# A hybrid encoder layer on one core: the order of all instructions moved from a hand-written interleaving to a list scheduler inside the kernel

## The chip, the cores and the metric

One NeuronCore of a Trainium2 chip runs the whole layer in one launch. The metric is the device time in microseconds (us). The engines are PE (TensorE, matrix products), DVE (VectorE), ACT (ScalarE), POOL (GpSimd) and SP (SyncE, which here only issues DMA transfers). Each engine runs its own instructions in the order in which they stand in the program and waits on semaphores for the others, so an instruction that waits holds up everything that stands behind it on its engine.

## The reference

A residual stream `x` of 256 rows by 4096 goes through one wide projection (16,592 columns). Its columns feed sixteen heads of an attention with a forget gate ("fox"), thirty-two heads of a recurrence ("rwkv"), and a gate; both head groups are gated, joined, projected again, added to the stream and normalised:

```
proj = einsum('bsd,dc->bsc', x, w_in)            # 4096 x 16592 weights
fox_out = softmax attention with summed log-forget gates        # 16 heads of 128
rw = rw + (rw_prev - rw) * mu_shift                              # one step of token shift
S_t = S_{t-1} diag(w_t) + (S_{t-1} a_t) b_t^T + v_t k_t^T ;  y_t = S_t r_t   # 32 heads of 64
h = concat([fox_out, rwkv_out]) * silu(z)
out = einsum('bsc,cd->bsd', h, w_out)            # 4096 x 4096 weights
x = layernorm(ALPHA * x + out, ln_gain, ln_bias)
```

All of it is float32, and the two large weight matrices alone are 339 MB that must come from memory once.

## The kernel before

**The big products.** A float32 product is made of three fast ones. `split` (L137 to L142) writes a weight tile of 128 x 1024 as a rounded high part on ACT (L140, `w...h`) and a remainder on DVE (L141, `w...l`). `mm` (L144 to L148) then multiplies high by high, low by high and high by low: three matmuls of 128x512 for each of two halves of the rows and for each 512 columns of the tile, so twelve matmuls for one weight tile. The high parts have four buffers, the remainders three, the raw tiles four. So the split of tile k+3 cannot write its remainder before PE has finished tile k, and must have written it before PE reaches tile k+3.

**The loops.** A pass n (eight of them) handles two fox heads and four rwkv heads in four blocks b of sixteen weight tiles (`block`, L245). The first block, n=0 and b=0, runs apart at the start with its own loads, together with the small `accl` products. Then comes the output projection, eight blocks b of sixteen tiles (L839 to L853, `oacc`, weight tiles `wo`).

**The small work.** Everything else (token shift, norms, softmax, and for each n the recurrence by chunks) runs as Python generators in the list `sides`. `slot()` moves each of them one step. `block` calls it after every six big matmuls (L254), and `yield` in a generator means "let one slot pass", so the interleaving is written by hand as numbers of slots (`W`, L43). In two other loops slots are taken with no big matmuls between them: while a block is being unloaded (L882), and while a head is not finished (L900). What is issued in such a loop stands in one run in each engine's program.

**The recurrence for one n** (`rwkv`, L505). `gp` (products over 64 rows, on half the array) is masked into `gb`; `gb` goes through memory (`nd`) and comes back as `Nb`; 31 rounds of `prod` (L578, a product) and `xc` (L581, a sum) solve a small triangular system on DVE; `xc` goes through memory (`td`) and comes back as `T`, which four DVE transposes put into `X`. Then for each of four chunks: `rh` on PE, `R` on DVE, `up` on PE (L652), `UV` on ACT, `sp` and `yp` on PE. The products `sp`, `yp`, `rh`, `gp`, `qt` and `xp` use a part of the array as a tile of its own; `up`, `fpt`, `fsp`, `fop`, `lp`, `np`, `vs` and `bkt` use the whole array.

**The order.** The tile framework holds program order where `keep_in_program_order` says so and may move the rest. The splits stand where `weights` (L238) calls `fetch`: at the start of each tile's matmuls it fills up to three tiles ahead.

**The end.** After the last block, `moments(m)` (L960) turns the row statistics into factors: BN_AGGR (L970), a square root on ACT (L972), then on DVE a reciprocal (L973) and four tiny operations up to `zd` (L977), a transpose on PE (`zp`), a copy on ACT, and the last products `wp` (L1001). `gain` (L867) multiplies the last 512 columns; it is issued after `zd` by `tc.issue_after(last)`.

## Time and profile before

| what | value |
|---|---|
| time, median of 3 runs | 1956.07 us (1955.14 to 1956.11) |
| the profiled execution's own time | 1955.92 us |
| its span, first to last instruction | 1954.0 us |
| PE busy | 1935.8 us, 99% |
| PE weight loads | 1585.4 us, 81% |
| DVE, ACT, POOL busy | 1366.9, 978.4, 79.9 us |
| moved by DMA | 420 MB, mean 215 GB/s |
| granted clock of PE, mean | 0.997 |

A row of a time line gives the start, the duration, engine, source line, operation, the tile written and the tiles read, and in brackets how long the engine was idle before it and who ended that. Durations of matmuls overlap, since they are pipelined: what a matmul costs is the distance from its start to the start of the next. `L146` is line 146 of the kernel before. A float32 product on the small side shows as two matmuls in the trace for one in the program.

### The profile page before, as it was taken

To read this page: it belongs to the slowest core of one execution; us is meant where nothing else is said; L and a number is where in the kernel's file an instruction comes from. 1 tells how busy PE (TensorE), PEld (TensorE's weight loads), DVE (VectorE), ACT (ScalarE), POOL (GpSimd) and SP (SyncE) were. 2 spreads that over 40 slices of the span, in tenths; PEclk is the share of its full clock that TensorE was granted. 3 is DMA by queue.
4 is the path that set the end of the run, shared out by engine and by line. 5 is a ranking of instruction groups with operands and counts; after the bars stand their busy time and mean duration, and the time that the engine had idled before them with its cause. 6 is when DMAs were issued, how large, how long until landed. Compare 5 with 4: busy or idle time off the path is not lost.

```text
span 1954.0 us, 28165 instructions
## 1 busy us (share of the span) xinstructions
PE 1935.8 (99%) x10153; PEld 1585.4 (81%) x10153; DVE 1366.9 (70%) x2212; ACT 978.4 (50%) x1485; POOL 79.9 (4%) x111
## 2 busy tenths in 40 slices
PE   9998999999999999999999999999999999999998
PEld 7887888878887888788878887888788878888886
DVE  6588667866886687667857785778577856755555
ACT  6453455455545554565456545644564454433332
POOL 0010001000100010001000100010001000000000
PEclk9999999999999999999999999999999999999999
DMA  9577767867785778677867786777677877866664
GB/s 337 146 235 198 208 167 241 225 194 199 226 234 184 215 213 233 193 219 208 225 195 219 212 226 194 227 211 219 193 228 203 269 259 241 251 199 200 189 198 168
DMA packets 269392, 420.13 MB, mean 215 GB/s; under 512 B 142338, under 2 KB 171028, under 8 KB 269252
## 3 DMA queue, kind: packets, MB, share of 16 engines
q1 hardware_dynamic: 268820, 417.91, 72.8%
q8 instruction: 80, 1.31, 0.3%
q14 instruction: 60, 0.49, 0.1%
q10 hardware_dynamic: 432, 0.43, 0.1%
HBM read 388.61 MB, written 29.64 MB: 214 GB/s over the span
## 4 chain that ended last, share of the span: by engine, by line
PE 95%; DVE 3%; DMA 1%; ACT 0%; issue 0%; DVEq 0%; SPq 0%; ACTq 0%
PE acc L146 24%; PE acc L148 23%; PE acc L147 23%; PE oacc L851 6%; PE oacc L853 6%; PE oacc L852 6%; PE yp L677 1%; PE gp L517 1%; PE up L652 1%; PE rh L625 1%; PE sp L661 0%; DVE xc L581 0%; DVE prod L578 0%; PE fsp L716 0%; PE fop L735 0%
## 5 line engine op out<-in xcount | busy, mean ns | idle before, releaser
L581 DVE TENSOR_REDUCE xc<-prod 128x8 f32<-128x16 f32 (+30 forms) x248 | 73.1, 295 | 7.1
L578 DVE TENSOR_TENSOR prod<-Nb,xc 128x8 f32<-128x8 f32 (+30 forms) x248 | 71.7, 289 | 6.4
L141 DVE TENSOR_TENSOR w_0l<-w,w_0h 128x1024 fp32r<-128x1024 f32 x31 | 38.2, 1232 | 37.7 <-ACT w_0h L140 27.4
L141 DVE TENSOR_TENSOR w_6l<-w,w_6h 128x1024 fp32r<-128x1024 f32 x31 | 39.0, 1258 | 34.8 <-ACT w_6h L140 18.7
L141 DVE TENSOR_TENSOR w_10l<-w,w_10h 128x1024 fp32r<-128x1024 f32 x31 | 37.9, 1224 | 36.1 <-PE acc L148 20.1
L141 DVE TENSOR_TENSOR w_8l<-w,w_8h 128x1024 fp32r<-128x1024 f32 x31 | 37.8, 1219 | 33.7 <-ACT w_8h L140 14.0
L140 ACT CAST w_0h<-w 128x1024 fp32r<-128x1024 f32 x31 | 32.7, 1054 | 55.0 <-DMA w<-in_w_main_dram 35.0
L141 DVE TENSOR_TENSOR w_5l<-w,w_5h 128x1024 fp32r<-128x1024 f32 x31 | 38.4, 1240 | 28.4 <-PE acc L148 17.3
L140 ACT CAST w_7h<-w 128x1024 fp32r<-128x1024 f32 x31 | 32.6, 1052 | 48.3 <-PE acc L147 28.8
L148 PE MATMUL acc<-w_7l,x 128*128 128x512 f32 x124 | 48.6, 400 | 5.8 <-DVE w_7l L141 5.8
L141 DVE TENSOR_TENSOR w_7l<-w,w_7h 128x1024 fp32r<-128x1024 f32 x31 | 37.9, 1222 | 21.9 <-PE acc L148 12.8
L141 DVE TENSOR_TENSOR w_11l<-w,w_11h 128x1024 fp32r<-128x1024 f32 x31 | 37.9, 1223 | 20.5 <-PE acc L148 14.9
L141 DVE TENSOR_TENSOR w_12l<-w,w_12h 128x1024 fp32r<-128x1024 f32 x31 | 37.5, 1211 | 19.5 <-PE acc L148 16.0
L140 ACT CAST w_13h<-w 128x1024 fp32r<-128x1024 f32 x31 | 32.6, 1052 | 37.1 <-DMA w<-in_w_main_dram 17.9
L146 PE MATMUL acc<-w_8h,x 128*128 128x512 f32 x124 | 50.5, 407 | 0.6 <-ACT w_8h L140 0.6
L146 PE MATMUL acc<-w_7h,x 128*128 128x512 f32 x124 | 51.0, 411 | 0.0
L146 PE MATMUL acc<-w_5h,x 128*128 128x512 f32 x124 | 50.5, 408 | 0.0
L141 DVE TENSOR_TENSOR w_14l<-w,w_14h 128x1024 fp32r<-128x1024 f32 x31 | 38.2, 1231 | 17.3 <-issue 10.9
L146 PE MATMUL acc<-w_3h,x 128*128 128x512 f32 x124 | 50.3, 405 | 0.0
L140 ACT CAST w_8h<-w 128x1024 fp32r<-128x1024 f32 x31 | 32.5, 1050 | 34.8 <-DMA w<-in_w_main_dram 24.5
L140 ACT CAST w_10h<-w 128x1024 fp32r<-128x1024 f32 x31 | 32.5, 1047 | 34.8 <-PE acc L147 32.6
L146 PE MATMUL acc<-w_6h,x 128*128 128x512 f32 x124 | 49.9, 402 | 0.0
(813 smaller groups left out, 6527.6 us busy)
## 6 DMA issues: line engine op xcount, KB each, us to landing
w<-in_w_main_dram SPq DMA_DIRECT2D x496, 512.0 KB, 3.9
wo<-in_w_o_dram SPq DMA_DIRECT2D x128, 512.0 KB, 3.8
bt<-bk SPq DMA_DIRECT2D x88, 128.0 KB, 4.2
Nb<-nd SPq DMA_DIRECT2D x16, 512.0 KB, 4.6
wr<-in_w_main_dram SPq DMA_DIRECT2D x15, 512.0 KB, 6.2
hd<-hl SPq DMA_DIRECT2D x29, 256.0 KB, 4.5
h<-hd SPq DMA_DIRECT2D x29, 256.0 KB, 5.6
raw<-bt SPq DMA_DIRECT2D x16, 256.0 KB
```

What stands on the lines that cost most here:

```text
L140: nc.scalar.copy(hi[:, :n], src[:, :n])
L141: nc.vector.tensor_tensor(lo[:, :n], src[:, :n], hi[:, :n].bitcast(F32), ALU.subtract)
L146: nc.tensor.matmul(acc[:, :n], xs[k][:, 0, tt], hi[:, o : o + n], start=(k == 0), stop=False)
L147: nc.tensor.matmul(acc[:, :n], xs[k][:, 1, tt], hi[:, o : o + n], start=False, stop=False)
L148: nc.tensor.matmul(acc[:, :n], xs[k][:, 0, tt], lo[:, o : o + n], start=False, stop=(k == KT - 1))
L517: nc.tensor.matmul(gp[u][j][:, c * P : (c + 1) * P], BK[h, u, c, :], lt[j][h, u, c, :], start=True, stop=True)
L578: first = nc.vector.tensor_tensor(prod[:, :, :, s + 1 :], nb[:, :, s : s + 1, s + 1 :].to_broadcast([P, 2, NJ, w]), xc[:, :, :, s + 1 :], ...
L581: nc.vector.tensor_reduce(xc[:, :, :, s : s + 1], prod[:, :, :, s:], AX.X, ALU.add)
L625: nc.tensor.matmul(rh[HALF[j], u * C : (u + 1) * C], lt[j][:, u, c, 0:C], SV[j][:, u, c, :], start=True, stop=True)
L851: nc.tensor.matmul(acc, ht[k][:, 0, tt], hi, start=(k == 0), stop=False)
L852: nc.tensor.matmul(acc, ht[k][:, 1, tt], hi, start=False, stop=False)
L853: nc.tensor.matmul(acc, ht[k][:, 0, tt], lo, start=False, stop=(k == KT - 1))
```

## The change

Every operation is now noted instead of issued. `nc` becomes an object `Later` whose engines record each call with its operands. `flush` then gives an order: it starts with estimated durations (`span_of`), goes forward in its own estimated time, and lets each engine take, among the operations that are ready and for which a buffer is free, the one with the lowest key. The key is the place in the program; for what `weights` notes (loads and splits of weights) it is lower by 100,000, so that these go first. Small matmuls become ready only 1000 ns after their inputs in the second of three flushes, which holds nearly all of the work. Matmuls that follow each other in the same partial-array tiling are kept together (`batches`). The instructions are then issued in that order, and `keep_in_program_order` holds each of them in it. The operations themselves, their operands, buffers and numbers are the same.

```diff
+SWITCH = 190
+MARGIN = 1000
...
+    def take(self, engine, call, name, args, kwargs):
...
+        op.hold, op.lag = span_of(engine, name, kwargs, outs[0], ins)
...
+        op.key = self.count - self.sooner
...
+        if engine == "tensor":
+            bank = outs[0].tensor.name
+            if bank in self.banks:
+                op.after.add(self.banks[bank])
+            self.banks[bank] = op
...
+    def flush(self, stay=(), closing=None, margin=0):
+        made = [o for o in self.ops]
+        ops, self.ops = self.batches(), []
...
+        def admit(op):
+            op.ready = max([0.0] + [self.seen(o, op) for o in op.after])
+            if op.engine == "tensor" and not op.main:
+                op.ready += margin
+            heapq.heappush(soon[op.engine], (op.ready, op.key, id(op), op))
...
+            _, _, op = heapq.heappop(ready[e])
+            if e == "tensor" and self.mode and op.mode != self.mode:
+                same = [x for x in ready[e] if x[2].mode == self.mode]
+                if same:
...
+            wait = self.places(op)
+            if wait is None:
+                held.append(op)
+                continue
...
+        made.sort(key=lambda o: o.start)
...
+        for op in made:
+            ins = op.call(*op.args, **op.kwargs)
+            self.tc.keep_in_program_order(ins)
...
+    def batches(self):
...
+                if op.mode and last and last.mode == op.mode:
+                    own = {id(o) for o in last.parts}
+                    if not any(any(id(b) in own for b in o.after) for o in op.after if o.engine != "tensor"):
+                        last.parts.append(op)
+                        continue
...
+    def places(self, op):
+        at = 0.0
+        for where in op.touches:
+            if self.left[where][3]:
+                continue
+            free, queue = self.slots[self.left[where][0]]
+            if not free or (len(free) < 5 and queue[0] != where and not self.left[where][0].startswith("ps")):
+                return None
+            at = max(at, free[0])
+        return at
...
-    nc = tc.nc
+    nc = Later(tc)
...
+    nc.flush(closing="_spool")
...
+        nc.sooner = AHEAD
         while len(ready) < 3 and (stream or raws):
             fetch()
+        nc.sooner = 0
...
+            nc.flush([t for _, *hl in ready for t in hl] + [raw for _, raw in raws], "_rp", MARGIN)
...
-    with tc.issue_after(last):
-        gain(0, NB - 1)
+    z0, _ = moments(0)
+    gain(0, NB - 1)
...
+    nc.flush()
```

`span_of` gives each operation an estimated time on its engine and a delay until its result can be used, from its engine, its shape and, for a transfer, its size and the size of its pieces. `admit` adds the margin to every small matmul, also to one whose only predecessor is the matmul before it in the same PSUM bank (`self.banks`).

## The prediction

> **What bounds the kernel now.** The page first: PE is busy nearly all of the span, and the chain that ended last runs along PE.

> ```profile
> span 1954.0 us, 28165 instructions
> ...
> PE 1935.8 (99%) x10153; PEld 1585.4 (81%) x10153; DVE 1366.9 (70%) x2212; ACT 978.4 (50%) x1485; POOL 79.9 (4%) x111
> ...
> PE 95%; DVE 3%; DMA 1%; ACT 0%; issue 0%; DVEq 0%; SPq 0%; ACTq 0%
> ```

> DVE at 70% and ACT at 50% are no bound on the average. So an order can win only what PE spends waiting, what it loses by how small matmuls lie between big ones, and the ends. The waits of PE by releaser say what waiting there is:

> ```profile
> PE acc L148 <- DVE w_7l L141: 5.8, 1, 5.8
> PE zp L989 <- DVE zd L977: 1.4, 1, 1.4
> PE warmup L108 <- POOL idle L105: 1.3, 1, 1.3
> PE acc L146 <- ACT w_8h L140: 0.6, 1, 0.6
> PE acc L148 <- DVE wr2l L141: 0.5, 1, 0.5
> PE oacc L853 <- DVE wo_3l L141: 0.5, 1, 0.5
> ```

> One wait is worth speaking of. PE's time line around it:

> ```profile
> 186.56 0.39 PE L146 MATMUL acc<-w_7h,x 128*128 128x512 f32 x1
> 192.71 0.80 PE L148 MATMUL acc<-w_7l,x 128*128 128x512 f32 x1 [5.75 <-DVE w_7l L141]
> 193.30 0.63 PE L147 MATMUL acc<-w_7h,x 128*128 128x512 f32 x1
> 193.72 0.63 PE L148 MATMUL acc<-w_7l,x 128*128 128x512 f32 x1
> ...
> 198.42 0.56 PE L147 MATMUL acc<-w_8h,x 128*128 128x512 f32 x1
> 198.81 0.40 PE L148 MATMUL acc<-w_8l,x 128*128 128x512 f32 x1
> ```

> After the wait the matmuls start 0.42 us apart. The windows view has the reason: the granted clock.

> ```profile
> 186.00:192.00 6.00, 0.95 (x5) 0.45 (x3) 5.62 (x14) 0.45 (x2) 0.00 (x0) 0.99 0.02 8
> 192.00:199.00 7.00, 6.29 (x15) 5.03 (x16) 3.68 (x5) 5.05 (x8) 0.00 (x0) 0.52 0.65 186
> ```

> The third number from the end of a row is the clock: 0.52 in the seven microseconds after the wait. DVE, which PE waited for, was busy 5.62 of the 6 us, with this between two splits:

> ```profile
> 178.98 1.22 DVE L141 TENSOR_TENSOR w_6l<-w,w_6h 128x1024 fp32r<-128x1024 f32 x1
> ...
> 190.50 0.42 DVE L581 TENSOR_REDUCE xc<-prod 128x8 f32<-128x256 f32 x1
> 190.84 0.68 DVE L564 TENSOR_TENSOR bon<-bon,vv 128x512 f32<-128x512 f32 x1
> 191.43 1.22 DVE L141 TENSOR_TENSOR w_7l<-w,w_7h 128x1024 fp32r<-128x1024 f32 x1
> ```

> For 12 us DVE worked off a run of `prod` and `xc` rounds, because the loop at L882 had issued them without big matmuls and so without splits between.

> **The change part by part.**

> *The splits (first key).* Before, at the end of this run of DVE in pass n=0, block 3 (`w_3_7l` is the remainder of its tile 7):

> ```order
> L578 TENSOR_TENSOR prod_1689<-Nb_1547,xc_1690 128x8x30
> L581 TENSOR_REDUCE xc_1690<-prod_1689 128x8
> L578 TENSOR_TENSOR prod_1689<-Nb_1547,xc_1690 128x8x31
> L581 TENSOR_REDUCE xc_1690<-prod_1689 128x8
> L564 TENSOR_TENSOR bon_1085<-bon_1085,vv_1818 128x512
> L141 TENSOR_TENSOR w_3_7l<-w_3_7_1804,w_3_7h 128x1024
> L141 TENSOR_TENSOR w_3_8l<-w_3_8_1834,w_3_8h 128x1024
> ```

> and now on DVE, the same place:

> ```order
> L358 TENSOR_TENSOR w_3_5l<-w_3_5_1031,w_3_5h 128x1024
> L358 TENSOR_TENSOR prod_1019<-Nb_993,xc_1020 128x8x19
> L358 TENSOR_REDUCE xc_1020<-prod_1019 128x8
> L358 TENSOR_TENSOR prod_1019<-Nb_993,xc_1020 128x8x20
> L358 TENSOR_REDUCE xc_1020<-prod_1019 128x8
> L358 TENSOR_TENSOR prod_1019<-Nb_993,xc_1020 128x8x21
> L358 TENSOR_TENSOR w_3_6l<-w_3_6_1034,w_3_6h 128x1024
> L358 TENSOR_REDUCE xc_1020<-prod_1019 128x8
> L358 TENSOR_TENSOR prod_1019<-Nb_993,xc_1020 128x8x22
> L358 TENSOR_REDUCE xc_1020<-prod_1019 128x8
> L358 TENSOR_TENSOR prod_1019<-Nb_993,xc_1020 128x8x23
> L358 TENSOR_TENSOR w_3_7l<-w_3_7_1038,w_3_7h 128x1024
> ```

> The rounds are spread among the splits. Over the whole program the longest run of other DVE operations between two splits falls from 28 to 11, and the 11 stand once, in the first blocks; elsewhere it is 8. So this wait goes. Its worth: from 186.56 to 192.71 is 6.15 us instead of one interval of 0.227 (rows below), so 5.92; from 192.71 to 198.81 there are fourteen intervals in 6.10 instead of 3.18 us, so 2.92. Together **-8.84 us**. I see nothing late next at this place: `w_3_6l` and `w_3_8l` are no further apart than elsewhere.

> [...]

> *The other small waits.* In the output projection the remainder came late by

> ```profile
> 1685.28 0.39 PE L852 MATMUL oacc<-wo_3h,h 128*128 128x512 f32 x1
> 1686.19 0.50 PE L853 MATMUL oacc<-wo_3l,h 128*128 128x512 f32 x1 [0.53 <-DVE wo_3l L141]
> ```

> 0.91 - 0.23 = 0.68 us, after the row statistics and `gain` of two blocks had been issued in a row; now splits stand between these. **-0.68**. The wait for `w_8h` (0.6) and the one for `wr2l` (0.5) lie in the first 100 us, where the first small chain and the first loads are; the new order has its run of 11 operations there, so I keep them: 0, at best -1.1.

> *The margin, and small matmuls one by one.* The margin also parts matmuls that only share a bank. On PE in pass 2, before, `up` (products of the recurrence) and the big `acc` products:

> ```order
> L148 MATMUL acc_0_1_5751<-w_0_2l,x_285 128x512
> L652 MATMUL up_0_5851<-R_0_5836,X 128x64 x2
> L146 MATMUL acc_0_0_5750<-w_0_2h,x_288 128x512
> L147 MATMUL acc_0_0_5750<-w_0_2h,x_288 128x512
> L148 MATMUL acc_0_0_5750<-w_0_2l,x_288 128x512
> ```

> and now:

> ```order
> L358 MATMUL up_0_1781<-R_0_1776,X 128x64
> L358 MATMUL acc_0_0_1764<-w_0_2l,x_154 128x512
> L358 MATMUL acc_0_1_1765<-w_0_2h,x_154 128x512 x2
> L358 MATMUL acc_0_1_1765<-w_0_2l,x_154 128x512
> L358 MATMUL acc_0_0_1764<-w_0_3h,x_159 128x512
> L358 MATMUL up_0_1781<-R_0_1776,X 128x64
> ```

> The pair has become two, five big matmuls apart. The same happens to `lp`, `np`, `vs`, `fsp`, `fpt`, `fop`, `tr` and, in twos, `bkt`: small matmuls stand in 467 places between big ones, 245 before. The partial-array groups (`gp`, `qt`, `xp`, `rh`, `sp`, `yp`) are whole in both. What a lone one costs against a group, PE's time line shows, since before has a few of both:

> ```profile
> 206.31 0.39 PE L148 MATMUL acc<-w_10l,x 128*128 128x512 f32 x1
> 206.54 0.49 PE L730 MATMUL fpt<-cs,lg 128*128 128x128 f32 x3
> 206.79 0.48 PE L146 MATMUL acc<-w_11h,x 128*128 128x512 f32 x1
> 207.10 0.39 PE L147 MATMUL acc<-w_11h,x 128*128 128x512 f32 x1
> 207.33 0.39 PE L148 MATMUL acc<-w_11l,x 128*128 128x512 f32 x1
> ```

> ```profile
> 399.11 0.39 PE L148 MATMUL acc<-w_10l,x 128*128 128x512 f32 x1
> ...
> 399.79 0.39 PE L148 MATMUL acc<-w_10l,x 128*128 128x512 f32 x1
> 400.02 0.27 PE L730 MATMUL fpt<-cs,lg 128*128 128x128 f32 x1
> 400.05 0.48 PE L146 MATMUL acc<-w_11h,x 128*128 128x512 f32 x1
> 400.37 0.39 PE L147 MATMUL acc<-w_11h,x 128*128 128x512 f32 x1
> ```

> 399.11 to 399.79 are three intervals, so 0.227 each. The three cost 207.33 - 206.31 - 3 x 0.227 = 0.34, that is 0.113 each; the lone one 400.37 - 399.79 - 2 x 0.227 = 0.126. So a place more costs about 0.013 us. With 222 places more: 2.9 us if all cost so; nothing, or 1 us less than nothing, if the 256 and 512 wide ones (`lp`, `np`, `vs`, most of the extra places) lose nothing by standing alone, which no row here settles. I take the middle, **+1.5**, from -1 to +2.9.

> As for the margin itself: `up` stood 6 big matmuls behind `rh` and now stands 8 behind, and the chunks of the recurrence lie further apart. That chain is not on the path, and each pass has room for it: X is made long before `qt` needs it.

> *The end.* `issue_after` is gone. On DVE, before:

> ```order
> L970 BN_AGGR mv_17445<-lst_855 128x2
> L973 RECIPROCAL rs_17447<-sd_17446 128x1
> L974 TENSOR_TENSOR s_17448<-mv_17445,rs_17447 128x1
> L975 CAST zh_17449<-s_17448 128x1
> L976 COPY zd_17450<-zh_17449 128x2
> L977 TENSOR_TENSOR zd_17450<-s_17448,zh_17449 128x1
> L867 TENSOR_TENSOR res_15549<-res_15549,lg_17231 128x512
> ```

> now:

> ```order
> L358 BN_AGGR mv_15900<-lst_839 128x2
> L358 TENSOR_TENSOR res_15549<-res_15549,lg_15857 128x512
> L358 RECIPROCAL rs_15902<-sd_15901 128x1
> L358 TENSOR_TENSOR s_15903<-mv_15900,rs_15902 128x1
> L358 CAST zh_15904<-s_15903 128x1
> ```

> `gain` now fills the gap in which DVE waited for ACT's square root, and is longer than it:

> ```profile
> 1942.59 0.37 DVE L970 BATCH_NORM_AGGREGATE mv<-lst 128x2 f32<-128x48 f32 x1
> 1943.32 0.16 DVE L973 RECIPROCAL rs<-sd 128x1 f32<-128x1 f32 x1 [0.36 <-ACT sd L972]
> ...
> 1944.12 0.68 DVE L867 TENSOR_TENSOR res<-res,lg 128x512 f32<-128x512 f32 x1
> ```

> 0.68 - 0.36 = 0.32 later for the reciprocal and all behind it: `zd`, PE's `zp`, ACT's copy, `wp`. For the second half of the rows that chain is the end of the kernel; for the first half PE reaches its `zp` with nothing to spare, and waits. Nothing needs `gain` earlier. Twice 0.32: **+0.6**; at least one of the two, at most both.

> *Noting, keys and program order* add no instruction: each engine has the same operations. Loads keep their depth of four raw tiles.

> The sum on the profiled execution's own 1955.92 us (span 1954.0 and 1.9 around it, 0.15 under the median): 1955.92 - 8.84 - 0.68 + 1.5 + 0.6 = **1948.5 us**. Its own range: 1955.92 - 8.84 - 0.68 - 1.1 - 1 + 0.3 = 1944.6 below, 1955.92 - 8.84 + 2.9 + 0.6 + 1.5 for small new waits = 1952.1 above.

> **The rivals.** *A wait takes the place of the old one.* In the first block DVE's run of 11 operations waits in turn for PE's first transposes, for ACT's copies and for a table load, and the split of tile 3 of block 1 stands behind it, with PE behind that. If PE idles there for 4 us and the half clock follows for 6.1 us (2.9 lost), 6.9 of the 9.5 us are given back: 1955.4 us. For it: the two waits that are there today. Against it stands the slack of the stretch now:

> ```profile
> 80.00:100.00 20.00, 19.07 (x82) 14.89 (x83) 13.68 (x22) 10.78 (x17) 0.00 (x0) 1.00 0.63 179
> ```

> DVE (the third of the five busy times) is free for 6.3 of the 20 us and ACT, the fourth, for 9.2, so they catch up. 0.13.

> *Slower: `X` waits for `T`.* After the last `xc` of a pass only three splits now stand before the transposes into `X`, where 11 to 16 stood: 3 x 12 x 0.227 = 8.2 us. The trip through memory took

> ```profile
> 396.53 0.90 SPq L588 DMA_DIRECT2D td<-xc  x2
> ...
> 400.93 3.65 SPq L590 DMA_DIRECT2D T<-td  x8
> ```

> ```profile
> T<-td SPq DMA_DIRECT2D x64, 16.0 KB, 1.7
> ```

> 400.93 + 3.65 + 1.7 - 396.53 = 9.75 us, so DVE may stand 1.5 us, and behind it the next split, for which PE waits. That split has two tiles of room, 5.4 us, less its own 1.2: PE waits when the trip passes some 12.4 us. SP is a queue too; the eight `T` loads may stand behind weight loads that wait for buffers. At 16 us PE would lose 3.6 us in each of eight passes, 28.8 us, and the clock with it: 1977 us or more. For it: the order. Against: 9.75. 0.10.

> *A lone small matmul is nearly free.* Its weights load while the big one before it runs. The row at 400.02 shows 0.03 us to the next start. If 0.03 were all, 222 places times 0.08 would give 18 us: 1929 us. The next row speaks against it: the big matmul behind starts 0.32 later instead of 0.227. [...] 0.04.

> That the order stays as it was is excluded: the rows above are the built programs.

> **How the numbers follow.** A measurement of this kernel tells about 0.2% from no change, 3.9 us: faster is under 1952.2, slower over 1960.0. The forecast has 0.73 and lies in faster with the last rival (0.04): 0.77. The moved wait is 0.13 in the middle, the slower rival 0.10. The range leaves out the last two rivals, 0.14: from 1944 to 1958, the upper end for a moved wait a little larger than priced. The forecast's own is 1944.6 to 1952.1.

> **What would show it.** Right: no PE wait over 1 us between 60 and 1900 us, the clock at 1.00 in every window there, no run of DVE over 4 us between splits, lone `fpt` at about 0.13, the reciprocal at the end 0.3 later behind `gain`. Wrong: a PE wait behind a split that stands behind `X`, or 0.5 in the clock column again; or `up` and `lp` places that cost well over 0.03 more than in groups; or a time over 1952.2.

## The result, and the profile after

The changed kernel takes 2019.9 us (median of 4) against 1955.8 before: ratio 1.0324, 95% interval 1.0311 to 1.0337. It is slower by 64 us, and the forecast of 1948.5 was wrong. Page of after, then the waits of PE by releaser (us in total, times, longest), and those of DVE for transfers:

```profile
span 2018.3 us, 28221 instructions
...
PE 1963.0 (97%) x10153; PEld 1593.9 (79%) x10153; DVE 1389.1 (69%) x2212; ACT 988.9 (49%) x1485; POOL 83.1 (4%) x111
```

```profile
PE fpt L358 <- DVE lg L358: 12.8, 6, 2.8
PE acc L358 <- DVE w_12l L358: 9.8, 6, 3.8
PE rh L358 <- DVE SV L358: 7.0, 5, 2.0
PE acc L358 <- DVE w_7l L358: 3.7, 4, 1.2
PE fsp L358 <- DVE lg L358: 3.3, 1, 3.3
PE oacc L358 <- ACT bk L358: 3.2, 1, 3.2
```

```profile
DVE X L358 <- DMA T<-td: 31.7, 8, 5.2
DVE prod L358 <- DMA Nb<-nd: 22.3, 8, 4.0
DVE bon L358 <- DMA vv<-vt: 11.2, 6, 2.5
```

Where one wait mattered before, PE now waits for many results of DVE and ACT, and DVE, which makes most of them, stands in front of round trips through memory for 65.2 us. Before, its only wait for a round trip was 0.9 us:

```profile
DVE w_12l L141 <- DMA T<-td: 0.9, 1, 0.9
```

One pass shows the chain. DVE of after in pass 2, end of the triangular rounds:

```profile
597.00 0.43 DVE L358 SCALAR_TENSOR_TENSOR zf<-f4t,zf 128x256 f32<-128x256 f32 x1 [1.37 <-ACT f4t L358]
...
601.79 0.41 DVE L358 TENSOR_REDUCE xc<-prod 128x8 f32<-128x256 f32 x1
602.12 1.21 DVE L358 TENSOR_TENSOR w_9l<-w,w_9h 128x1024 fp32r<-128x1024 f32 x1
603.25 1.22 DVE L358 TENSOR_TENSOR w_10l<-w,w_10h 128x1024 fp32r<-128x1024 f32 x1
...
606.40 1.21 DVE L358 TENSOR_TENSOR w_11l<-w,w_11h 128x1024 fp32r<-128x1024 f32 x1
607.53 0.41 DVE L358 TENSOR_REDUCE fst<-lg 128x1 f32<-128x256 f32 x1
612.78 0.43 DVE L358 STREAM_TRANSPOSE X<-T 32x256 f32<-32x256 f32 x1 [4.83 <-DMA T<-td]
613.14 0.11 DVE L358 RECIPROCAL fst<-fst 128x1 f32<-128x1 f32 x1
613.28 0.43 DVE L358 STREAM_TRANSPOSE X<-T 32x256 f32<-32x256 f32 x1
613.75 1.23 DVE L358 TENSOR_TENSOR w_12l<-w,w_12h 128x1024 fp32r<-128x1024 f32 x1
614.89 0.35 DVE L358 TENSOR_SCALAR lg<-lg,fst 128x256 f32<-128x256 f32 x1
```

ACT and PE at that time:

```profile
596.55 0.42 ACT L358 ACTIVATE f4t<-zf 128x256 f32<-128x256 f32 x1 [0.30 <-DMA zf<-bt]
```

```profile
611.82 0.63 PE L358 MATMUL acc<-w_11h,x 128*128 128x512 f32 x2
615.29 0.33 PE L358 MATMUL fpt<-cs,lg 128*128 128x128 f32 x1 [2.84 <-DVE lg L358]
615.38 0.48 PE L358 MATMUL acc<-w_11l,x 128*128 128x512 f32 x1
```

`X` waits 4.83 us for `T`; behind it on DVE stand the reciprocal and the product of a softmax (`fst`, `lg`) and a split; PE has `fpt`, which reads `lg`, in the middle of tile 11 and stops 2.84 us, with all its big matmuls behind. The rows show it: `w_11l` was written at 607.61, and its next matmul starts at 615.38, behind `fpt` at 615.29.

From the starts of PE's matmuls the span divides like this (us, of the profiled executions; a wait is a start over 0.3 late behind a big matmul; half clock is what big matmuls at 0.43 instead of 0.227 lose; the rest is small matmuls and what big ones lose beside them; what is missing to the span, some 1749 us, is the big matmuls at one interval each). Five of the 29 late starts come without idle time of PE, at half clock just behind a wait, and so does one of the six before:

| | waits | half clock | rest | span |
|---|---|---|---|---|
| before | 8.8 (6) | 5.7 | 189.9 | 1954.0 |
| after | 48.4 (29) | 17.2 | 204.1 | 2018.3 |
| after, every trip 2 + 2 us longer in the plan | 3.0 (3) | 5.6 | 193.4 | 1951.4 |
| the same 4 + 4 us, no margin in a bank | 2.1 (3) | 4.1 | 188.8 | 1944.3 |

### The profile page after: what moved, and what is told of

The parts are those of the page before. It is cut to its first block, busy times and chain, and to the rows that moved or that the text cites. A ratio compares the mean times of both kernels' runs of the same rounds, so it can differ in the third digit from the quotient of the medians.

```text
span 2018.3 us, 28221 instructions
## 1 busy us (share of the span) xinstructions
PE 1963.0 (97%) x10153; PEld 1593.9 (79%) x10153; DVE 1389.1 (69%) x2212; ACT 988.9 (49%) x1485; POOL 83.1 (4%) x111
## 5 line engine op out<-in xcount | busy, mean ns | idle before, releaser
L358 DVE TENSOR_TENSOR prod<-Nb,xc 128x8 f32<-128x8 f32 (+30 forms) x248 | 71.9, 290 | 28.5 <-DMA Nb<-nd 22.3
L358 PE MATMUL acc<-w_12h,x 128*128 128x512 f32 x248 | 83.2, 415 | 0.0
L358 PE MATMUL acc<-w_4h,x 128*128 128x512 f32 x248 | 81.6, 403 | 0.0
L358 PE MATMUL acc<-w_7h,x 128*128 128x512 f32 x248 | 81.0, 399 | 0.0
L358 PE MATMUL acc<-w_0h,x 128*128 128x512 f32 x248 | 79.0, 396 | 1.7 <-ACT vt L358 1.1
L358 PE MATMUL acc<-w_9h,x 128*128 128x512 f32 x248 | 80.5, 403 | 0.0
L358 PE MATMUL acc<-w_3h,x 128*128 128x512 f32 x248 | 80.5, 397 | 0.0
L358 PE MATMUL acc<-w_11h,x 128*128 128x512 f32 x248 | 80.4, 403 | 0.0
L358 PE MATMUL acc<-w_2h,x 128*128 128x512 f32 x248 | 79.6, 398 | 0.0
L358 PE MATMUL acc<-w_8h,x 128*128 128x512 f32 x248 | 79.1, 399 | 0.0
L358 PE MATMUL acc<-w_6h,x 128*128 128x512 f32 x248 | 78.5, 394 | 0.0
L358 PE MATMUL acc<-w_5h,x 128*128 128x512 f32 x248 | 78.0, 396 | 0.0
L358 PE MATMUL acc<-w_14h,x 128*128 128x512 f32 x248 | 77.5, 390 | 0.0
L358 PE MATMUL acc<-w_13h,x 128*128 128x512 f32 x248 | 77.3, 393 | 0.0
L358 PE MATMUL acc<-w_15h,x 128*128 128x512 f32 x248 | 77.3, 393 | 0.0
L358 DVE TENSOR_REDUCE xc<-prod 128x8 f32<-128x16 f32 (+30 forms) x248 | 73.0, 294 | 6.2
L358 PE MATMUL acc<-w_1h,x 128*128 128x512 f32 x248 | 76.8, 391 | 0.0
L358 PE MATMUL acc<-w_10h,x 128*128 128x512 f32 x248 | 76.8, 390 | 0.0
L358 PE MATMUL acc<-w_12l,x 128*128 128x512 f32 x124 | 51.9, 418 | 9.8 <-DVE w_12l L358 9.8
L358 ACT CAST w_7h<-w 128x1024 fp32r<-128x1024 f32 x31 | 32.5, 1048 | 52.7 <-DMA w<-in_w_main_dram 25.2
L358 DVE TENSOR_TENSOR w_15l<-w,w_15h 128x1024 fp32r<-128x1024 f32 x31 | 37.6, 1212 | 29.3 <-PE acc L358 15.9
L358 PEld LDWEIGHTS acc<-w_12h,x 128*128 128x128 f32 x248 | 48.7, 199 | 10.2
```

The lines of the kernel that those rows point to most:

```text
L358: ins = op.call(*op.args, **op.kwargs)
```

## The experiments

All are the changed kernel with an edit; times are medians, ratios are to before. Theory A: the planner takes round trips through memory as shorter than they are; its order is fixed, so DVE and ACT stand in front of them. B: putting splits first delays the small work. C: the margin is too short.

**Every trip longer in the plan** (`trips`). Nothing runs longer by this; the order changes.

```diff
         late = 2300 if out.space != bass.MemoryType.DRAM else 2800
+        if not str(ins[0].tensor.name).startswith("in_"):
+            late += 2000
```

> In this run the planner reckons 2 us more for every transfer into memory and 2 us more for every transfer back out of it (weights and inputs as they were), so whatever waits for a round trip is put later in the order. Between the last xc and X five splits now stand on DVE instead of three, between gb and prod five instead of four. Theory A (DVE and ACT stand in front of round trips that last longer than planned, and PE runs dry behind them): of the 48.4 us in 29 PE waits over 0.3 us fewer than 12 stay, of the 17.2 us at half clock fewer than 6, so 2019.9 - 36 - 11 = 1973 us, from 1960 to 1980. Theory B (splits go first and make the small DVE work late): nothing about that changes, 2010 to 2025. Theory C (the margin in front of small matmuls is too short): 2010 to 2025 as well.

1956.35 us, ratio 1.0002 (0.9993 to 1.0012): 63.5 us back, where A had 40 to 60 and B and C at most 10. In the table waits and half clock give back 57.0 us instead of the 47 expected, and the rest 10.7 more; what these 10.7 are was not taken apart. DVE of this run, pass 2:

```profile
576.78 0.42 DVE L360 TENSOR_REDUCE xc<-prod 128x8 f32<-128x256 f32 x1
577.42 1.23 DVE L360 TENSOR_TENSOR w_10l<-w,w_10h 128x1024 fp32r<-128x1024 f32 x1 [0.22 <-PE acc L360]
...
583.65 1.22 DVE L360 TENSOR_TENSOR w_12l<-w,w_12h 128x1024 fp32r<-128x1024 f32 x1
586.31 1.23 DVE L360 TENSOR_TENSOR w_13l<-w,w_13h 128x1024 fp32r<-128x1024 f32 x1 [1.43 <-issue]
589.42 1.23 DVE L360 TENSOR_TENSOR w_14l<-w,w_14h 128x1024 fp32r<-128x1024 f32 x1 [1.88 <-ACT pT L360]
590.56 1.83 DVE L360 STREAM_TRANSPOSE X<-T 32x256 f32<-32x256 f32 x4
```

Five splits and the whole softmax stand ahead of `X` now, and `X` waits for nothing. In front of `prod` DVE still waits for `Nb`, 12.4 us in eight passes (22.3 in the change as it stood), but five splits stand ahead there too, and PE's waits for `w_12l` are gone: a stop of DVE cost PE next to nothing here once enough of its work for PE stood ahead of it.

**Trips shorter in the plan** (`late -= 1000`, `short1`).

> The change with 1 us less for each leg of the round trips than it reckons (only the planner's number; nothing on the chip is made faster). Theory A: each of some five trips in each pass makes DVE or ACT stop up to 2 us longer, and where PE was waiting already all of that goes through: 8 x 5 x 0.6 to 1.5 us, so 2045 to 2080. If the waits come from anything else than the trips, it stays near 2020.

2063.2 us, ratio 1.0549 (1.0529 to 1.0568): the dose goes both ways. DVE's waits grow as its orders move up:

```profile
DVE prod L360 <- DMA Nb<-nd: 51.7, 8, 8.1
DVE X L360 <- DMA T<-td: 34.2, 8, 6.0
```

**One trip alone** (the edit for names that begin with `td`, or with `nd`).

> The planner reckons 2 us more for each of the two legs of one round trip alone, xc through td into T; five splits then stand between the last xc and X instead of three. Theory A by its parts: of the waits of after, fpt behind X (six, 13.8 us by the distance of starts) goes, with some 3 us of half clock: 2019.9 - 17 = 2003 us, 1997 to 2010. The other round trips (nd, vt, bt) keep their waits. Rival (the slower rival of the prediction is all there is to it: T delays everything behind it): 1955 to 1970 us.

2005.6 us: as A has it, 14.3 of the 64 us; the `fpt` waits went.

> The planner reckons 2 us more for each leg of the round trip of gb through nd into Nb alone. Theory A by its parts: the waits for w_12l (six over 0.3 us, 10.7 us), which stand behind prod, and the half clock behind two of them (3.4 us) go; one more split comes in front of X as well, so a part of the fpt waits too: 2019.9 - 14 = 2006 us, from 1993 if the fpt waits go with them. Rival (Nb delays everything behind it in the pass): 1955 to 1975 us.

1985.8 us: 34.1 us, where A by parts had 14 to 27. The waits for `w_12l` and for `fpt` both went, but DVE's own stops at `Nb` hardly got shorter:

```profile
DVE prod L360 <- DMA Nb<-nd: 17.6, 8, 5.0
```

What changed is the order around the stops: five splits instead of four stand ahead of `prod`, four instead of three ahead of `X` (from pass 1 on), and DVE's wait in front of `X` fell from 31.7 to 10.5 us. So the parts don't stand alone, and this run is no measure of one trip by itself; that a stop at `Nb` makes DVE late for what follows in the pass fits, but was not shown apart from the new order. The rival, one trip as the whole cause, fails both times. The trips through `vt`, `bt` and `hd` were not lengthened alone; they are the likely place of the rest.

**Splits not first** (`AHEAD = 0`).

> The key of loads and splits of weights is their place in the program here, nothing subtracted. Three splits still stand between the last xc and X. Theory B (splits first make lg, SV and shl late): the 28 us that PE waits in front of small matmuls go, and with them half of the half clock: about 1980 us. Theory A (round trips longer than planned): no change beyond 10 us, 2010 to 2030. Theory C: the same.

2007.2 us: 12.7 us less than the change as it stood, a little more than the 10 that A allowed and far from the 40 of B. 45.6 us of waits in 34 places stay, so splits first is not the main cause.

**No margin inside a bank, and a longer margin.**

```diff
-            op.ready = max([0.0] + [self.seen(o, op) for o in op.after])
-            if op.engine == "tensor" and not op.main:
-                op.ready += margin
+            late = margin if op.engine == "tensor" and not op.main else 0
+            op.ready = max([0.0] + [self.seen(o, op) + (late if o.engine != "tensor" else 0) for o in op.after])
```

> The margin is added only behind results of other engines, no longer between matmuls of one PSUM bank: small matmuls stand in 242 places between big ones instead of 466. In the trace of after, each change from a small 64 or 128 wide matmul to a big one shows 0.09 us more than an interval (up x64, fpt x43, bkt x24, fsp, fop, tr) and the excess outside waits and half clock is 14 us above before. If standing alone is what costs this: 2019.9 - 14 = 2006 us. If it costs what I took in the forecast, 1.5 us: 2018. The waits of theory A stay in either case, since the order around the round trips stays; theory B and C say the same of them.

1992.6 us (1988 to 2006): 27 us less where the larger expectation was 14. In the profiled execution, whose span is 29.8 us shorter, some 11 us each are waits and half clock and 8 the rest.

> As the run without margin inside a bank, and the margin is 3000 ns instead of 1000. Theory C (the margin is too short): the PE waits in front of small matmuls (28 of 48.4 us) go and with them most of the half clock: about 35 us below the run with 1000 ns, near 1971. Theory A (DVE and ACT stop at round trips): waits of up to 3.5 us are covered for the small matmuls alone, but the splits behind the stop stay late (w_12l, w_7l, 16 of 48.4 us) and new work comes later: 10 to 25 us below the run with 1000 ns. Theory B: the same as A or less.

1979.4 us, 13 below the run with 1000 ns. It covers small matmuls; the splits behind a stop stay late:

```profile
PE acc L357 <- DVE w_12l L357: 7.3, 6, 2.9
PE sp L357 <- ACT UV L357: 5.5, 4, 2.3
PE oacc L357 <- ACT bk L357: 4.0, 1, 4.0
```

This is within what A had (10 to 25) and not the 35 of C. Both margin edits together give back 40.5 of the 64 us without touching the trips, by letting small matmuls stand behind the stops; a margin over 3000 ns was not run. So C treats a symptom.

**What the parts are worth once trips are long enough.**

> Both edits: 2 us more for each leg of all round trips, and the margin only behind results of other engines (242 places of small matmuls instead of 466). If standing alone costs what the comparison of after with the run without margin in a bank shows outside of waits and half clock (8.1 us): 1956.35 - 8 = 1948 us. If it costs what the forecast took (1.5, at most 2.9 us): 1955, at least 1953.5.

> As the run with both edits, with 4 us more for each leg instead of 2. Theory A: when no engine stops in front of a round trip any more, more delay brings nothing: within 3 us of the run with 2 us. If trips still last longer than planned somewhere, 2 to 4 us faster. If the recurrence has no room for the later start (gp to the last yp of a pass), slower by more than 5 us.

> 6 us more for each leg, margin not inside a bank. Theory A: nothing left to gain, within 3 us of 1946.2. If the recurrence runs out of room in a pass: slower by 5 us or more, with waits in front of rh or up.

> 4 us more for each leg of all round trips, and the margin as it was (465 places of small matmuls): against 1946.2 us with 242 places this is the price of standing alone, with hardly a wait in either. From the traces with 2 us (small matmuls and what the big ones lose beside them: 193.4 us with 466 places, 190.0 with 242) it is 3.4 us: 1949.6 us. By the forecast's 1.5: 1947.7; by the 8.1 us of the comparison with waits: 1954.

> The best version so far with the key of loads and splits not lowered. If splits first does nothing once the trips are reckoned long enough: within 3 us of 1946.2. If splits first is what keeps PE from waiting for splits: slower by 5 us or more, with waits for w in PE's list. If it costs (theory B in a small way): faster by 3 us or more.

| plan | small matmuls by one | together (no margin in a bank) |
|---|---|---|
| 2 + 2 us | 1956.35 | 1954.5 |
| 4 + 4 us | 1955.7 | 1946.2 |
| 6 + 6 us | not run | 1949.2 |

1946.2 beats both kernels: ratio 0.9953 (0.9937 to 0.9970). Neither edit does so alone (1955.7 with 4 + 4 us, 1992.6 with no margin in a bank). With both edits at 2 + 2 us the time was that of the forecast's small price (1955), not 1948, and there were still waits for `shl` (6.1 us in four); going to 4 + 4 us won 8.3 us where I had expected 2 to 4 at most. 4 + 4 us with the margin as it was came out above all three expectations (1947.7 to 1954). 6 + 6 is 3 us slower by the medians, at the edge of what I had expected, and the intervals of the ratios overlap (0.9952 to 0.9979). Without splits first it is 1948.6 (0.9963, 0.9950 to 0.9977): no clear difference. PE's waits in the best run:

```profile
PE zp L359 <- DVE zd L359: 1.5, 1, 1.5
PE warmup L359 <- POOL idle L359: 1.3, 1, 1.3
PE up L359 <- ACT f15t L359: 0.9, 1, 0.9
PE np L359 <- DVE shl L359: 0.5, 1, 0.5
```

The price of standing alone stays between two numbers: 1.9 us by the first row, 9.4 by the second (expected 3.4). In the traces with 4 + 4 us the median lone matmul costs little more than its share of a group (`lp` 0.130 for 0.119, `fpt` 0.121 for 0.113); with the margin as it was the trace shows waits in front of lone ones beside that (`fsp` up to 1.8 us). How much of the 9.4 is which was not taken apart.

## Why the prediction was wrong

**The step that failed** is that the sum holds no term for DVE's stops in front of round trips. I had one such stop, as the slower rival "`X` waits for `T`", gave it 0.10 and let it cost PE nothing below a trip of 12.4 us. In its place DVE stood 65.2 us at three trips, PE's waits grew by 39.6 us, its half clock by 11.5 and the rest by 14.2. The rival's mechanism was there; its conditions were wrong in three ways.

- I let three splits cover 8.2 us, a tile of PE's pace each. DVE was late: in the planner's own start times the last `xc` ends 3.6 us before PE begins tile 8, on the chip 0.4 us after. Ahead of that on DVE lie the stop at `Nb` (2.25 us) and one at 597.00 for `zf` (1.37 us), whose input came late to ACT from a trip of its own. So it did the splits one behind the other: from 602.20, where the last `xc` ends, it was done by 607.94, with the softmax work among them. The trip took 612.78 - 602.35 = 10.4 us, near my 9.75, and DVE stood 4.83 us instead of 1.5.
- I named the next split as what stands behind, with two tiles of room, and so a trip of 12.4 us as the point where it decides. Behind `X` stood `fst` and `lg`, and PE's `fpt` has no room: only the margin, 1 us.
- I looked at one trip. `prod` behind `Nb` went from five splits to four, which the prediction does not price; `bon`, `zf` and `fq` have trips too. PE was late 29 times, and with longer trips in the plan 3 of these are left. For `gb` the planner's own start times have 12.8 us from the first store to the first `prod`; the chip took 565.78 - 550.71 = 15.1 in pass 2, and 14.5 to 18.2 in passes 1 to 7. For `T` they have 9.2 us to the first `X`, and the chip took 9.0 to 10.9: that trip was planned nearly right, so of the 4.83 us in pass 2 some 1.2 are the trip being longer than planned, and most of the others DVE having come late to it. The first stores of the two trips, and the end of the first trip:

```profile
550.71 3.68 SPq L358 DMA_DIRECT2D nd<-gb  x8
...
602.35 0.87 SPq L358 DMA_DIRECT2D td<-xc  x2
```

```profile
565.78 0.18 DVE L358 TENSOR_TENSOR prod<-Nb,xc 128x8 f32<-128x8 f32 x1 [2.25 <-DMA Nb<-nd]
```

The planner's delays could have been laid beside the trace of before, trip by trip; I did that for `T` alone, and there against PE's pace and not the plan.

**The old stall (-8.84).** The wait of 5.75 us went, but from 192.31 on PE now waited 3.35 us for `lg`, and half clock followed. With longer trips in the plan 0.6 us stays there, with 4 + 4 us nothing: the term was right for an order in which DVE is not late.

**`wo_3l` (-0.68).** That wait went; another of 3.2 us (`oacc` for ACT's `bk`, in the list above) came at the start of the output projection. **The moved wait in the first block (rival at 0.13)** did not come: between 20 and 190 us nothing that stands behind a big matmul starts over 0.3 us late.

**Small matmuls one by one (+1.5, from -1 to +2.9).** The runs leave 1.9, inside my range, to 9.4 us, three times its upper end. A lone `fpt` costs 0.13 as predicted (610.78 to 611.59 is 0.81 for three intervals of 0.227):

```profile
610.78 0.39 PE L358 MATMUL acc<-w_10l,x 128*128 128x512 f32 x1
611.01 0.27 PE L358 MATMUL fpt<-cs,lg 128*128 128x128 f32 x1
611.04 0.71 PE L358 MATMUL acc<-w_11h,x 128*128 128x512 f32 x2
611.59 0.40 PE L358 MATMUL acc<-w_11l,x 128*128 128x512 f32 x1
```

I priced what it costs to stand alone, and not that each place more is a place more to wait at; how much of the 9.4 that is stays open. "Not on the path" was said of the chain; on PE a small matmul whose input was late held up the big ones behind it, for 2.84 us in pass 2.

**The end (+0.6).** 0.10 each instead of 0.32: from BN_AGGR to the reciprocal it takes 0.83 us, 0.73 before. `gain` started at 2007.16, before BN_AGGR had ended at 2007.24.

```profile
2006.87 0.37 DVE L358 BATCH_NORM_AGGREGATE mv<-lst 128x2 f32<-128x48 f32 x1
2007.16 0.63 DVE L358 TENSOR_TENSOR res<-res,lg 128x512 f32<-128x512 f32 x1
2007.70 0.15 DVE L358 RECIPROCAL rs<-sd 128x1 f32<-128x1 f32 x1
```

## What to carry to other kernels

An order made from estimates can turn an estimate that is too short into a stop of a whole engine, at every repetition (in front of `prod` and of `X` eight times each here, 22.3 and 31.7 us), and an engine that is late once can stop longer at the next trip (4.83 us in front of `X` in pass 2, of which some 1.2 are the trip being longer than planned); 2 us more for each leg than in the best run cost about 3 us here, hardly clear of the spread, 1 us less than in the change as it stood cost 43. So lay the planner's delay of every transfer beside the trace, and err on the long side. When an order is read, look at each instruction that waits for a transfer: how much of its engine's own time (not of its consumer's pace) lies ahead of it, what stands behind it, and who reads that.

## What was new about the hardware

In the trace of after a wait of 2.03 us was followed by half clock, and one of 2.84 us was not: what sets the two apart here is where the wait fell on a grid that the clock column of this trace shows. The eight stretches at 0.50 between 20 and 2000 us begin at 194.29, 310.35, 364.96, 412.75, 846.24, 1177.33, 1426.51 and 1641.55; the first lasts 6.83 us, the others 3.41 each. From the first start to the last it is 1447.26 us, and the distances between them are 34, 16, 14, 127, 97, 73 and 63 times 3.413 us, 424 times in all. These are windows on that grid (PE's busy time stands first behind the length, the clock third from the end); the waits were 2.16 us up to 364.81, 2.03 up to 411.34, and 2.84 up to 615.29:

```profile
361.55:364.96 3.41, 1.25 (x6) 0.71 (x6) 2.77 (x11) 1.71 (x2) 0.00 (x0) 1.00 0.40 161
364.96:368.37 3.41, 3.41 (x9) 2.64 (x10) 3.13 (x11) 0.38 (x1) 0.00 (x0) 0.50 0.52 154
409.33:412.75 3.42, 1.41 (x8) 1.15 (x8) 3.30 (x6) 0.07 (x1) 0.00 (x0) 1.00 0.55 158
412.75:416.16 3.41, 3.41 (x10) 2.69 (x9) 1.96 (x2) 1.52 (x2) 0.00 (x0) 0.50 0.78 232
610.72:614.13 3.41, 1.73 (x8) 1.03 (x7) 1.29 (x4) 1.04 (x1) 0.00 (x0) 1.00 0.77 183
614.13:617.55 3.42, 2.26 (x11) 1.86 (x12) 3.31 (x6) 0.62 (x2) 0.00 (x0) 1.00 0.49 158
```

The forecast and its rivals reckon with half clock only behind waits of 3.6 us and more; here it followed waits of 2.16 and 2.03.
